# Local attention with two query tiles in two column halves of the array, and sums of squares taken from the loaded rows

## The chip, the cores and the metric

The kernel runs on one core of a Trainium2 chip. The metric is the device time of one execution in microseconds. The kernel before takes 3316.08 us (median of 3 runs, 3313.69 to 3317.71).

## The reference

Two layers of a trunk over 1024 latent tokens with a prefix of 256 context tokens, width 1024, all in float32. Each layer: a modulated RMS norm; one input projection; three mixers side by side (latent attention with 6 heads, a bidirectional state space model, and local attention); an output projection with a gated residual; a second modulated norm and a gated feed-forward part with a convolution. The modulation is silu(c) times the large matrix w_mod.

Two pieces matter here.

The norm: `x * rsqrt(mean(x*x) + eps) * (1 + sc) + sh`, where the mean runs over the 1024 columns of a token.

The local attention: 6 query heads share 2 key-value heads (3 each), head size 64. A query tile of 128 tokens sees its own key tile, the tile before and the one behind (with a mask by distance), the 256 context keys, and a sink: one more logit in the denominator. Context queries see the context alone, in layer 0 only. So `out = sum(p * v) / (sum(p) + exp(sink))` over 5 key tiles (4 at the two ends; 2 for context queries).

## The kernel before, in words

The kernel is one function, `trunk`, written for a scheduler that puts the instructions of each engine in an order by priority and by its own model of time, allocates the tiles, and sets all waits. Tokens are in three chunks: 512, 512, and the 256 context tokens (`CHUNKS`). A helper `mm` issues each matmul, so every product stands at L86; every operation of VectorE and ScalarE stands at L55; transposes at L96. A float32 product is two records of TensorE in the profile (two passes); products of the rounded type fp32r are one.

**Pacing.** Side work runs as generators (`Side`), each advanced by a share of its steps per step of the main work: preparation of the next group, the state space model, the modulation vectors, loads of weights. So side work is tied to the count of attention steps and not to time.

**Local attention** (`swa_steps`). Per chunk and key-value head there is one group: 4 query tiles of 128 tokens, 3 heads side by side as 384 columns. The groups are the context chunk with both heads (layer 0 alone), then (0,0), (0,1), (1,0), (1,1) as (chunk, head). For each query tile and each key tile, a step: two or three products give the scores with keys on the partitions and 384 query columns (`ka`/`qa` and `kb`/`qb` hold rounded parts, so that together they are exact enough; the third adds the mask), ScalarE takes the exponential into `p` (`sp` in the profile), and a function `av`, run two steps later, multiplies with the values: `v1` is 128 keys by 65 columns, of which the last is all ones. Row 65 of the result is the sum of the probabilities. PSUM has 3 banks for scores (`s`), 3 for side work (`b`), 2 for `av`. Behind the last key tile ScalarE copies the 64 rows to `num` and the 65th to `den`, and after the head's last tile `swa_norm` sends the sums through DRAM, adds the sink, inverts, and multiplies.

While a group runs, the next one is prepared (`swa_prep`: transposes, and a maximum of scores per query by VectorE, `smx`); layer 0 also computes a modulation vector (`mod_gen`, `macc`) on VectorE; from step 16 on the mixer's outputs and the output weights are loaded and split into rounded halves (`load_split`). The last group of a layer has no preparation beside it. The output projection (`o`) follows.

**The beginning.** `prep_x(ci)` transposes a chunk of the loaded rows (`xin`) into `xs` (features on partitions). Beside it `norm_stats` squares the transposed tiles on ScalarE, adds them on VectorE (`nb`) and sums over partitions by products with ones (`f<-ones,nb`); GpSimd takes the power -1/2. `use_wm(k)` multiplies the k-th block of w_mod, on TensorE (`pr`) and on VectorE (`x<-wm`, accumulated); `load_wm` loads blocks two ahead, through SP's queue, into 6 buffers. Behind the eighth block `s1_weights(0)` issues three loads of w_in and splits each on ScalarE and VectorE (`wh`, `wl`); there are two buffers for the raw loads. Then the shift `h1` and the scale `A1` are finished, applied, and the first input projections (`tk`) run.

Of the kernel before, what the change touches and what calls it, by code (L numbers as in the profile page):

```python
# [19 lines left out]
D = 1024  # L20
# [12 lines left out]
def trunk(ctx, tc, x, c, ctxt, c_ctx, w_mod, b_mod, norm1, w_in, q_lora_g, w_uq, kv_lora_g, w_ukv,  # L33
# [84 lines left out]

    def stt(out, a, s, b, op0=ALU.mult, op1=ALU.add):
        V.scalar_tensor_tensor(out, a, s, b, op0=op0, op1=op1)  # L120
# [5 lines left out]
    def load_split(hi, lo, raw, srcs, scale=None):  # L126
# [3 lines left out]
        if scale is None:  # L130
            act(hi, raw)
            sub(lo, raw, f32(hi))
        else:
            act(hi, raw, AF.Copy, scale=scale)
            stt(lo, raw, scale, f32(hi), ALU.mult, ALU.subtract)
# [290 lines left out]
    big = [pp.tile([128, 1024], F32, name=f"nb{i}") for i in range(2)]  # L426
    pr = prp.tile([2, 1536], F32, name="pr")
    acc = [[xs[2 * z + q][:, 512:1024] for q in range(2)] for z in range(2)]

    def prep_x(ci):  # L430
        t0, n = CHUNKS[ci]
        st = norm_stats(big, pp, fps, xs, ci, rn[:, ci])
        for k in range(8):
            ps = fps()
            for i in range(n // 128):
# [5 lines left out]
            next(st)  # L441
            yield
        for _ in st:
            yield
# [57 lines left out]
    wS1 = s1_weights(0)  # L502
# [206 lines left out]
    for l in range(2):  # L709
# [969 lines left out]
        def swa_steps(ci, kv):  # L1679
# [9 lines left out]
            for i in range(nt):  # L1689
                t = tt0 + i  # L1690
                kts = [(8, None), (9, None)]
                if ci < 2:
                    kts = [(kt, None if kt == t else (0 if kt < t else 1))
                           for kt in range(max(t - 1, 0), min(t + 2, NL))] + kts
                cs = slice(off + i * 384, off + (i + 1) * 384)
                box = {}
                for e, (kt, mk) in enumerate(kts):
                    ps = cps.tile([128, 512], F32, tag="s", name="s", bufs=3)[:, 0:384]
                    ks = slice(kt * 128, (kt + 1) * 128)
                    mm(ps, ka[:, ks], qa[:, cs], True, False)  # L1700
                    mm(ps, kb[:, ks], qb[:, cs], False, mk is None)
                    if mk is not None:
                        mm(ps, swa["ident_r"], swa["mask_r"][:, mk:mk + 1, :].to_broadcast([128, 3, 128]), False, True)
                    p = swp.tile([128, 384], F32, tag="p", name="sp", bufs=4)
                    act(p, ps, AF.Exp, scale=0.125)

                    def av(e=e, kt=kt, p=p, i=i, box=box, last=e == len(kts) - 1):
# [471 lines left out]
```

## Time and profile before

| | |
|---|---|
| median of the runs | 3316.08 us |
| the profiled execution | 3317.35 us |
| its span | 3315.5 us |
| TensorE, busy | 3216.9 us (97%) |
| VectorE, busy | 2259.5 us (68%) |
| ScalarE, busy | 1160.0 us (35%) |
| GpSimd, busy | 108.1 us (3%) |
| mean granted TensorE clock | 0.985 |

Engines in the rows: PE is TensorE's matmuls, PEld its weight loads, DVE VectorE, ACT ScalarE, POOL GpSimd, SP the queue that issues transfers. A matmul's duration includes its latency, so back-to-back matmuls overlap in the records; their rate is read from the distance of their starts. `x8` in a row of the timeline is 8 instructions in a row, with the time from the first start to the last end.

### The profile page before, as it was taken

To read this page: it belongs to the slowest core of one execution; us is meant where nothing else is said; L and a number is where in the kernel's file an instruction comes from. 1 tells how busy PE (TensorE), PEld (TensorE's weight loads), DVE (VectorE), ACT (ScalarE), POOL (GpSimd) and SP (SyncE) were. 2 spreads that over 40 slices of the span, in tenths; PEclk is the share of its full clock that TensorE was granted. 3 is DMA by queue.
4 is the path that set the end of the run, shared out by engine and by line. 5 is a ranking of instruction groups with operands and counts; after the bars stand their busy time and mean duration, and the time that the engine had idled before them with its cause. 6 is when DMAs were issued, how large, how long until landed. Compare 5 with 4: busy or idle time off the path is not lost.

```text
span 3315.5 us, 41986 instructions
## 1 busy us (share of the span) xinstructions
PE 3216.9 (97%) x15950; PEld 2582.9 (78%) x15950; DVE 2259.5 (68%) x4076; ACT 1160.0 (35%) x2078; POOL 108.1 (3%) x99
## 2 busy tenths in 40 slices
PE   8999699999999999999999999999999999999999
PEld 5897466677878888888888888556668788888888
DVE  7656898885687776666666945887644755565565
ACT  4542344555242222222222553445562322222221
POOL 0220000000000000000000122000000000000000
PEclk9999799999999999999999999999999999999999
DMA  8434221434312222222211445111323112111111
GB/s 268 124 94 109 68 77 49 115 100 147 105 53 76 61 80 65 63 73 65 74 61 36 126 119 141 33 43 40 88 76 113 39 48 61 45 39 58 51 38 58
DMA packets 401892, 263.16 MB, mean 79 GB/s; under 512 B 173711, under 2 KB 370457, under 8 KB 401689
## 3 DMA queue, kind: packets, MB, share of 16 engines
q1 hardware_dynamic: 401042, 260.20, 27.1%
q8 instruction: 126, 2.06, 0.2%
q14 instruction: 77, 0.63, 0.1%
q10 hardware_dynamic: 647, 0.26, 0.0%
HBM read 207.41 MB, written 50.66 MB: 78 GB/s over the span
## 4 chain that ended last, share of the span: by engine, by line
PE 81%; DVE 12%; DMA 3%; ACT 2%; issue 1%; POOL 1%; SPq 1%; DVEq 0%; ACTq 0%; POOLq 0%
PE u L86 32%; PE d L86 11%; PE av L86 6%; PE dx L86 5%; PE o L86 5%; PE f L86 5%; PE tk L86 5%; PE s L86 5%; PE b L86 4%; PE b L96 2%; DVE mx L55 1%; DVE macc L55 1%; DVE cm L55 1%; DMA mw<-in_w_mod_dram 1%; DVE al L55 1%
## 5 line engine op out<-in xcount | busy, mean ns | idle before, releaser
L86 PE MATMUL u<-ah,wh 128*128 128x512 f32 (+1 forms) x1760 | 651.0, 370 | 4.0 <-ACT ah L55 2.2
L86 PE MATMUL u<-al,wh 128*128 128x512 f32 (+1 forms) x1760 | 649.6, 369 | 1.4 <-DVE al L55 1.4
L86 PE MATMUL u<-ah,wl 128*128 128x512 f32 (+1 forms) x1760 | 649.1, 369 | 0.0
L55 ACT ACTIVATE wh<-raw 128x1024 fp32r<-128x1024 f32 (+3 forms) x184 | 189.3, 1036 | 720.4 <-PE d L86 292.2
L55 DVE SCALAR_TENSOR_TENSOR cv<-u,par,cv 128x511 f32<-128x511 f32 (+2 forms) x616 | 326.0, 555 | 135.6 <-ACT cv L55 130.4
L86 PEld LDWEIGHTS u<-ah,wh 128*128 128x128 f32 x1760 | 332.5, 189 | 60.6 <-ACT ah L55 3.1
L86 PEld LDWEIGHTS u<-al,wh 128*128 128x128 f32 x1760 | 332.8, 189 | 57.7 <-DVE al L55 2.0
L86 PEld LDWEIGHTS u<-ah,wl 128*128 128x128 f32 x1760 | 332.6, 189 | 55.5
L55 DVE TENSOR_TENSOR wl<-raw,wh 128x1024 fp32r<-128x1024 f32 (+3 forms) x184 | 218.4, 1191 | 173.0 <-ACT wh L55 171.9
L55 DVE SCALAR_TENSOR_TENSOR x<-d,g,x 128x512 f32<-128x512 f32 (+2 forms) x307 | 209.4, 685 | 109.1 <-PE d L86 108.8
L55 ACT ACTIVATE cv<-u,par,par 128x512 f32<-128x512 f32 (+1 forms) x220 | 159.7, 728 | 323.2 <-PE u L86 320.8
L86 PE MATMUL av<-p,v 128*65 128x512 f32 (+1 forms) x504 | 255.6, 590 | 1.2 <-ACT den L55 0.8
L55 DVE SCALAR_TENSOR_TENSOR macc<-mw,srow,macc 128x256 f32<-128x256 f32 (+1 forms) x364 | 187.2, 539 | 65.4 <-DMA mw<-in_w_mod_dram 64.2
L86 PE MATMUL d<-ah,wh 128*128 128x512 f32 (+2 forms) x614 | 224.5, 366 | 1.3 <-DVE x L55 1.2
L86 PE MATMUL d<-al,wh 128*128 128x512 f32 (+2 forms) x614 | 223.5, 364 | 0.0
L86 PE MATMUL d<-ah,wl 128*128 128x512 f32 (+2 forms) x614 | 223.4, 364 | 0.0
L55 ACT ACTIVATE p<-s 128x512 f32<-128x512 f32 (+1 forms) x252 | 147.4, 586 | 196.5 <-PE s L86 191.8
L55 DVE TENSOR_REDUCE mx<-b 128x1 f32<-128x512 f32 (+1 forms) x300 | 164.1, 586 | 35.6 <-PE b L86 34.2
L86 PE MATMUL s<-qh,kh 97*128 97x512 f32 (+1 forms) x252 | 157.4, 625 | 0.0
L86 PE MATMUL av<-sp,sv 128*65 128x384 f32 x320 | 127.3, 486 | 6.0 <-ACT sden L55 3.3
L55 DVE SCALAR_TENSOR_TENSOR x<-dx,g,x 128x512 f32<-128x512 f32 (+2 forms) x141 | 97.3, 690 | 51.4 <-PE dx L86 51.4
L86 PEld LDWEIGHTS d<-ah,wh 128*128 128x128 f32 x614 | 115.8, 189 | 20.7 <-DVE x L55 2.9
(346 smaller groups left out, 6157.7 us busy)
## 6 DMA issues: line engine op xcount, KB each, us to landing
raw<-in_w_up_dram SPq DMA_DIRECT2D x88, 512.0 KB
mw<-in_w_mod_dram SPq DMA_DIRECT2D x224, 128.0 KB
raw<-in_w_down_dram SPq DMA_DIRECT2D x44, 512.0 KB
mw<-in_w_mod_dram SPq DMA_DIRECT2D x48, 256.0 KB
wm<-in_w_mod_dram SPq DMA_DIRECT2D x16, 512.0 KB
xd<-x SPq DMA_DIRECT2D x32, 256.0 KB
raw<-in_w_in_dram SPq DMA_DIRECT2D x14, 512.0 KB
sqd<-sqb SPq DMA_DIRECT2D x36, 192.0 KB
```

Of the source, the lines that this page charges most:

```text
L55: return fn(out, *args, **kw)
L86: PE.matmul(out, lhsT, rhs, start=start, stop=stop)
L96: PE.transpose(out, in_, ident[0:p, 0:p])
```

## The change

Three edits.

1. `swa_steps` takes the query tiles of a group in pairs. For each place e in the two lists of key tiles it computes the scores of both tiles; the product with the values of the first tile goes to rows 0 to 63 of one PSUM bank, that of the second to rows 64 to 127 (64 columns of values each, without the ones). The sums of probabilities are made apart: `tot` is added up per query tile, the first tile's on VectorE, the second's on GpSimd, and behind the last key tile two products with ones give both denominators in another `av` bank. Where one list is longer, its last place goes alone. The buffers of `p` go from 4 to 5.
2. `prep_x` no longer uses `norm_stats`. ScalarE squares the loaded rows with a running sum along the row (`accum_out`), at k = 0 and k = 4; behind k = 4 two small operations and the power give the norm.
3. The loads of `s1_weights(0)` are issued behind block 3 of w_mod instead of behind the last; their splits are kept in a list and issued behind block 6.

```diff
@@ -116,6 +116,8 @@
         else:
             (eng or V).tensor_scalar(out, a, s1, s2, op0=op0, op1=op1)
 
+    later_splits = None
+
     def stt(out, a, s, b, op0=ALU.mult, op1=ALU.add):
         V.scalar_tensor_tensor(out, a, s, b, op0=op0, op1=op1)
 
@@ -127,9 +129,10 @@
 
         for dst, src in srcs:
             nc.sync.dma_start(out=dst, in_=src)
-        if scale is None:
-            act(hi, raw)
-            sub(lo, raw, f32(hi))
+        if later_splits is not None:
+            later_splits.append(lambda: split(hi, lo, raw))
+        elif scale is None:
+            split(hi, lo, raw)
         else:
             act(hi, raw, AF.Copy, scale=scale)
             stt(lo, raw, scale, f32(hi), ALU.mult, ALU.subtract)
@@ -424,23 +427,32 @@
     stt(th, th, 1.0, cv, ALU.add, ALU.mult)
     ts(srow.rearrange("p k j -> p j k"), th, 0.5)
     big = [pp.tile([128, 1024], F32, name=f"nb{i}") for i in range(2)]
+    xss = pp.tile([128, 2, NT], F32, name="xss")
     pr = prp.tile([2, 1536], F32, name="pr")
     acc = [[xs[2 * z + q][:, 512:1024] for q in range(2)] for z in range(2)]
 
     def prep_x(ci):
+
         t0, n = CHUNKS[ci]
-        st = norm_stats(big, pp, fps, xs, ci, rn[:, ci])
+        nt = n // 128
         for k in range(8):
+            if k % 4 == 0:
+                for i in range(nt):
+                    act(big[1][:, (i % 2) * 512:(i % 2) * 512 + 512], xin[t0 // 128 + i, k // 4], AF.Square,
+                        accum_out=xss[:, k // 4, t0 // 128 + i:t0 // 128 + i + 1])
             ps = fps()
-            for i in range(n // 128):
+            for i in range(nt):
                 tr(ps[:, i * 128:(i + 1) * 128], xin[t0 // 128 + i, k // 4][:, k % 4 * 128:k % 4 * 128 + 128])
             if k % 2:
                 V.tensor_copy(xs[k][:, t0:t0 + n], ps[:, :n])
             else:
                 act(xs[k][:, t0:t0 + n], ps[:, :n])
-            next(st)
-            yield
-        for _ in st:
+            if k == 4:
+                v = pp.tile([128, 4], F32, tag="nv", name="nv", bufs=2)
+                sl = slice(t0 // 128, t0 // 128 + nt)
+                add(v[:, :nt], xss[:, 0, sl], xss[:, 1, sl])
+                ts(v[:, :nt], v[:, :nt], 1.0 / D, EPS)
+                rsqrt_pool(rn[:, ci, 0:nt], v[:, :nt], nt)
             yield
 
     def use_wm(k):
@@ -499,7 +511,13 @@
         use_wm(k)
         if k + 2 < 8:
             load_wm(k + 2)
-    wS1 = s1_weights(0)
+        if k == 3:
+            later_splits = []
+            wS1 = s1_weights(0)
+            first_splits, later_splits = later_splits, None
+        if k == 6:
+            for fn in first_splits:
+                fn()
     load_x(1)
     load_x(2)
     rb0 = pp.tile([128, 256], F32, name="rb0")
@@ -1686,34 +1704,64 @@
             num, den = pair["snum"], pair["sden"]
             o = kv * 64
             tt0, nt = CHUNKS[ci][0] // 128, CHUNKS[ci][1] // 128
-            for i in range(nt):
-                t = tt0 + i
-                kts = [(8, None), (9, None)]
-                if ci < 2:
-                    kts = [(kt, None if kt == t else (0 if kt < t else 1))
-                           for kt in range(max(t - 1, 0), min(t + 2, NL))] + kts
-                cs = slice(off + i * 384, off + (i + 1) * 384)
+
+            def scores(i, kt, mk):
+                ps = cps.tile([128, 512], F32, tag="s", name="s", bufs=3)[:, 0:384]
+                ks, cs = slice(kt * 128, (kt + 1) * 128), slice(off + i * 384, off + (i + 1) * 384)
+                mm(ps, ka[:, ks], qa[:, cs], True, False)
+                mm(ps, kb[:, ks], qb[:, cs], False, mk is None)
+                if mk is not None:
+                    mm(ps, swa["ident_r"], swa["mask_r"][:, mk:mk + 1, :].to_broadcast([128, 3, 128]), False, True)
+                p = swp.tile([128, 384], F32, tag="p", name="sp", bufs=5)
+                act(p, ps, AF.Exp, scale=0.125)
+                return p
+
+            for i0 in range(0, nt, 2):
+
+                kts = []
+                for t in (tt0 + i0, tt0 + i0 + 1):
+                    r = [(8, None), (9, None)]
+                    if ci < 2:
+                        r = [(kt, None if kt == t else (0 if kt < t else 1))
+                             for kt in range(max(t - 1, 0), min(t + 2, NL))] + r
+                    kts.append(r)
+                ne = max(len(r) for r in kts)
+                tot = [None, None]
                 box = {}
-                for e, (kt, mk) in enumerate(kts):
-                    ps = cps.tile([128, 512], F32, tag="s", name="s", bufs=3)[:, 0:384]
-                    ks = slice(kt * 128, (kt + 1) * 128)
-                    mm(ps, ka[:, ks], qa[:, cs], True, False)
-                    mm(ps, kb[:, ks], qb[:, cs], False, mk is None)
-                    if mk is not None:
-                        mm(ps, swa["ident_r"], swa["mask_r"][:, mk:mk + 1, :].to_broadcast([128, 3, 128]), False, True)
-                    p = swp.tile([128, 384], F32, tag="p", name="sp", bufs=4)
-                    act(p, ps, AF.Exp, scale=0.125)
-
-                    def av(e=e, kt=kt, p=p, i=i, box=box, last=e == len(kts) - 1):
-                        if "av" not in box:
+                for e in range(ne):
+                    ps_ = []
+                    for z in range(2):
+                        if e >= len(kts[z]):
+                            continue
+                        kt, mk = kts[z][e]
+                        p = scores(i0 + z, kt, mk)
+                        ps_.append((z, kt, p, e == len(kts[z]) - 1))
+                        eng = G if z else V
+                        if e == 0:
+                            tot[z] = p
+                        else:
+                            q = tot[z]
+                            if e == 1:
+                                tot[z] = swp.tile([128, 384], F32, tag=f"tot{z}", name="stot")
+                            add(tot[z], q, p, eng)
+                        if z == 0 and len(kts[1]) > e:
+                            yield lambda: None
+
+                    def av(e=e, ps_=ps_, box=box, tot=tot, i0=i0, ne=ne):
+                        if e == 0:
                             box["av"] = cps.tile([128, 512], F32, tag="av", name="av", bufs=2)[:, 0:384]
                         av = box["av"]
-                        mm(av[0:65], v1[:, kt, :], p, e == 0, last)
-                        if last:
-                            sl = slice(i * 128, (i + 1) * 128)
-                            act(num[o:o + 64, :, sl], av[0:64, :].rearrange("p (h q) -> p h q", h=3))
-                            act(den[o:o + 1, :, sl], av[64:65, :].rearrange("p (h q) -> p h q", h=3))
-                            if kv == 1 and i == nt - 1:
+                        for z, kt, p, last in ps_:
+                            mm(av[64 * z:64 * z + 64], v1[:, kt, 0:64], p, e == 0, last)
+                        if e == ne - 1:
+                            dn = cps.tile([128, 512], F32, tag="av", name="sdn", bufs=2)[:, 0:384]
+                            for z in range(2):
+                                mm(dn[64 * z:64 * z + 64], ones[:, 0:64], tot[z])
+                            for z in range(2):
+                                sl = slice((i0 + z) * 128, (i0 + z + 1) * 128)
+                                act(num[o:o + 64, :, sl], av[64 * z:64 * z + 64, :].rearrange("p (h q) -> p h q", h=3))
+                                act(den[o:o + 1, :, sl], dn[64 * z:64 * z + 1, :].rearrange("p (h q) -> p h q", h=3))
+                            if kv == 1 and i0 == nt - 2:
                                 swa_norm(ci, num, den)
                     yield av
 
```

## Rows read from the trace of the kernel before

**Rows 1.** The page: busy time of the engines, and the chain that ended last.
```profile
PE 3216.9 (97%) x15950; PEld 2582.9 (78%) x15950; DVE 2259.5 (68%) x4076; ACT 1160.0 (35%) x2078; POOL 108.1 (3%) x99
...
PE 81%; DVE 12%; DMA 3%; ACT 2%; issue 1%; POOL 1%; SPq 1%; DVEq 0%; ACTq 0%; POOLq 0%
```
**Rows 2.** Busy by stretch: length, PE, PEld, DVE, ACT, POOL; clock, DMA, GB/s.
```profile
690.00:772.00 82.00, 78.70 (x397) 59.34 (x396) 70.70 (x168) 50.76 (x110) 0.00 (x0) 1.00 0.40 120
772.00:799.40 27.40, 26.87 (x111) 16.82 (x110) 8.73 (x19) 18.32 (x39) 0.00 (x0) 1.00 0.22 64
2377.00:2457.00 80.00, 79.63 (x389) 59.65 (x388) 51.71 (x108) 50.89 (x105) 0.00 (x0) 1.00 0.25 74
2457.00:2483.40 26.40, 24.23 (x100) 15.21 (x98) 4.90 (x5) 18.01 (x37) 0.00 (x0) 1.00 0.33 95
...
50.00:100.00 50.00, 45.78 (x301) 42.56 (x300) 43.89 (x106) 29.55 (x85) 4.93 (x5) 0.91 0.66 208
```
**Rows 3.** TensorE's timeline, layer 0, last group: start us, length, instruction.
```profile
742.49 0.33 PE L86 MATMUL s<-qb,kb 128*128 128x384 f32 x1
742.66 0.27 PE L96 MATMUL b<-ident,snm 128*12 128x128 f32 x1
742.77 0.81 PE L86 MATMUL av<-sp,sv 128*65 128x384 f32 x2
...
743.59 0.34 PE L86 MATMUL s<-qb,kb 128*128 128x384 f32 x1
743.76 0.34 PE L86 MATMUL s<-mask_r,ident_r 128*128 128x384 f32 x1
743.94 0.81 PE L86 MATMUL av<-sp,sv 128*65 128x384 f32 x2
```
**Rows 4.** The tile sp: durations in ns (min/median/max), first and last start.
```profile
L86 PE MATMUL av<-sp,sv x320: 483/485/537, 683.6 to 2483.4; 128*65 128x384 f32 x160
L55 ACT ACTIVATE sp<-s x160: 465/491/502, 682.1 to 2482.0; 128x384 f32<-128x384 f32 x160
```
**Rows 5.** TensorE's timeline: products with 64 rows; transposes with all rows.
```profile
367.83 0.60 PE L86 MATMUL b<-cv,bb 64*16 64x128 f32 x8
...
368.37 0.64 PE L96 MATMUL b<-ident,qn 128*96 128x128 f32 x4
...
689.68 1.03 PE L96 MATMUL b<-ident,q 128*128 128x128 f32 x8
```
**Rows 6.** VectorE: groups in 690 to 772 (busy, mean ns | idle); a stretch.
```profile
L55 DVE TENSOR_TENSOR snum<-snum,sden 128x512 f32<-128x512 f32 x3 | 1.9, 685 | 0.0
L55 DVE TENSOR_TENSOR snum<-snum,sden 128x256 f32<-128x256 f32 x3 | 1.2, 418 | 0.0
...
660.00:683.00 23.00, 23.00 (x113) 16.11 (x113) 21.83 (x55) 8.99 (x19) 0.00 (x0) 1.00 0.26 77
```
**Rows 7.** GpSimd: groups over the whole span.
```profile
L102 POOL TENSOR_TENSOR rinv<-ssq,mhalf 128x12 f32<-128x12 f32 x28 | 71.7, 2561 | 167.3 <-DVE ssq L55 167.3
L1257 POOL MEMSET Sg<- 64x4 f32 x16 | 1.6, 100 | 0.6
```
**Rows 8.** The beginning: two stretches, chain, groups of 0 to 100, timeline.
```profile
20.00:25.00 5.00, 4.01 (x22) 2.02 (x20) 3.82 (x7) 1.23 (x2) 0.00 (x0) 1.00 0.97 388
25.00:30.00 5.00, 5.00 (x19) 1.60 (x19) 4.58 (x12) 0.00 (x0) 1.18 (x1) 1.00 0.55 155
...
33.53 6.59 DMA wm<-in_w_mod_dram
...
L55 DVE TENSOR_TENSOR nb<-nb,nb 128x512 f32<-128x512 f32 x12 | 7.9, 685 | 2.1 <-ACT nb L55 2.0
...
L86 PE MATMUL f<-ones,nb 128*128 128x2 f32 x40 | 5.0, 243 | 1.0 <-DVE nb L55 1.0
...
L55 ACT ACTIVATE nb<-x x24: 402/624/633, 9.2 to 88.5; 128x512 f32<-128x512 f32 x16, 128x256 f32<-128x256 f32 x8
...
42.94 1.05 DVE L55 TENSOR_TENSOR wl<-raw,wh 128x864 fp32r<-128x864 f32 x1
```

## The prediction

> **What bounds the kernel now.** Begin with the page: TensorE is busy 97% of the span and holds 81% of the chain that ended last [rows 1]. So a change pays where it shortens TensorE's stream, as long as no other engine is full there. The parts touched are the local attention (682 to 799.4 us in layer 0, 2377 to 2483.4 us in layer 1) and the first 100 us. Next the table of stretches [rows 2]: read for each which engine comes second. TensorE is nearly full in all four attention stretches, but VectorE has 70.7 of 82 us in layer 0 at 690 to 772 and 51.7 of 80 us in layer 1 at 2377 to 2457; the last quarter of each stage has little VectorE and much ScalarE (18.3 of 27.4, 18.0 of 26.4 us). Last the order of TensorE's work [rows 3]: one step (one key tile of one query tile) with a mask takes 743.94 - 742.77 = 1.17 us; its three one-pass streams start 0.17 to 0.18 us apart, so the product with the values keeps 1.17 - 3 x 0.175 = 0.645 us. It is the dear half of the step: two records of 0.485 us latency each [rows 4], 320 records for 160 products, 103.2 us in all.
>
> **Products and sums, TensorE.** A latent group (one key-value head, four query tiles) has 5+5+5+4 = 19 products, 19 x 0.645 = 12.3 us. After the change the tiles go in pairs with lists of 4 and 5, or 5 and 5: 10 slots of up to two half-array products. Each pair adds one slot for its denominators (ones times the summed probabilities): 12 slots. Is a slot 0.645 us or twice that? No row has column halves, but one has row halves: products with 64 rows, alternating between the two halves, go 8 in 0.60 us; a record of 128 columns lasts 0.27 us [rows 3], so they start (0.60 - 0.27)/7 = 0.05 us apart, against (1.03 - 0.27)/7 = 0.11 us for full-array float32 passes of the same 128 columns [rows 5]. So two float32 products, both passes of each, ran side by side on different parts. I take a column slot at 0.645 us, the same as one product now; the bounds are 0.645 and 1.29. Then a group saves 12.3 - 12 x 0.645 = 4.5 us, eight groups 36, the two context groups (4 products to 3 slots each) 1.3: 37 us of TensorE's stream.
>
> Changing the shape of the array twice per slot: around the 12-column transpose the starts are 0.17 and 0.11 us apart, just its neighbour's and its own stream, so no gap [rows 3]; I take 0, and as the upper end 0.09 us, from the 64-row products: the last of the eight starts at 367.83 + 0.60 - 0.27 = 368.16 and the next full-array pass at 368.37, 0.21 where 0.11 is the stream [rows 5]. The Trainium skill (TensorEngine Tiling (Array Packing), Key Properties) says that changing the mode drains TensorE; the 64-row rows agree, the 12-column rows do not. By the page some 84 visits to the halves would cost 2 x 0.09 us each, 15 us of TensorE, and the sum below would lose about 8 of them, where TensorE sets the pace.
>
> **What the sums cost elsewhere.** Probabilities are now added per query tile: even tile on VectorE, odd tile on GpSimd, one add fewer than key tiles. VectorE's two-input operations in this stage take 0.685 us for 512 columns and 0.418 for 256 [rows 6]; 384 lie half way, 0.55 us. A latent group has 3+4 or 4+4 on VectorE, so three groups 22 x 0.55 = 12.1 us. For GpSimd there is no such row: its two-input operations (powers) are 2.56 us for 12 columns, memsets 0.10 us [rows 7]; these are the bounds, and I take about 1 us, between them, because a plain add is nearer the memset than the power. ScalarE has the same exponentials (0.491 us [rows 4]) and as many evacuations; only now four of these come in a row at a pair's end. Nothing else moves: the count of steps that paces loads, modulation and the next group's preparation is again 19 per group.
>
> **The stretches, one by one** [rows 2]. Layer 0, 690 to 772 (three groups beside preparation and modulation): TensorE 78.7 - 13.5 = 65.2, but VectorE 70.7 + 12.1 = 82.8 us. It would be full; the fullest stretch before it has 21.8 of 23 us, 95% [rows 6], so 82.8 to 87; I take 85, 3 us longer than now. Layer 0, 772 to 799.4 (one group, little beside it): TensorE 26.9 - 4.5 = 22.4, ScalarE 18.3: about 23.4, 4 less. Layer 1, 2377 to 2457 (no modulation): TensorE 79.6 - 13.5 = 66.1, VectorE 51.7 + 12.1 = 63.8; two engines nearly even do not pack perfectly, I take 70, 10 less. Layer 1's last group: TensorE 24.2 - 4.5 = 19.7, ScalarE 18.0: 21.4, 5 less. Together -16 us, though TensorE loses 37: VectorE eats the rest in layer 0. The output projection that follows is on TensorE alone and simply starts earlier.
>
> **The beginning.** The sums of squares leave VectorE (12 adds of 512 columns, 7.9 us, and 6 of 256) and TensorE (40 products with ones, 5.0 us of busy time); the eight squares of a chunk stay on ScalarE, now read from the loaded rows with a running sum, at about the 0.62 us that 512 columns cost now [rows 8]. ScalarE has 29.6 of 50 us at 50 to 100 [rows 2], so these hide; if the running sum costs 0.2 us more each, 20 of them are 4 us there, still hidden. Early on VectorE frees w_mod's buffers: transfers fall from 388 GB/s at 20 to 25 us to 155 at 25 to 30, because no buffer is free while VectorE adds squares. With these adds gone, up to 5 x (0.388 - 0.155) = 1.2 MB move earlier, some 3 us. Against it, two of the three w_in loads (128 x 864 float32, 0.44 MB, each) pass in SP's queue ahead of the last w_mod loads, whose landing ends the 6.59 us wait at 33.53 [rows 8]: 0.9 MB, 2.3 us at 0.388 MB/us. These two about cancel; bounds -3 and +3. The third w_in load still needs a buffer that the first split frees, now at step 6 and not after step 7. What is left is the two splits of 1.05 us that stand on VectorE between the reductions at 42 to 46 us, ahead of A1: 2.1 us sooner, in the wait for w_mod, where VectorE is idle. I take -3 us. At 50 to 100 us TensorE has 45.8 of 50 us [rows 2]: 24 of the 40 products with ones, 3 us, go. Beginning: -6 us, between +2 and -9.
>
> **Sum.** The profiled execution took 3317.35 us (span 3315.5), 1.3 us above the median of the runs, 3316.08. 3317.35 - 16 - 6 = 3295 us. Own range 3287 to 3304.
>
> **Rivals.**
> 1. The column halves run one after the other (the slower side). Then a group has 19 + 4 = 23 products of 0.645, 2.6 us more; eight groups 21, context 2.6, less 6 at the beginning: about 3335. It decides from a slot price of (103.2 + 6)/102 = 1.07 us on. For: no row shows column halves. Against: the row halves overlap fully [rows 5].
> 2. The overlap is half: of first and second passes only one pair meets, 0.96 us a slot, and back-to-back slots somewhat less. TensorE saves about 13 us, the stretches 4 plus 6: 3307.
> 3. TensorE waits at each pair's end for the odd tile's last add. Behind the last score come two products and two scores, 2 x 0.645 + 0.7 = 2.0 us; the exponential takes 0.5, so a GpSimd add up to 1.4 us is covered; at 2.5 us, its upper bound, 18 pair ends wait 1.1 us each: 20 us, so 3315. Behind the waiting product on TensorE stand all next scores, and for them wait the exponentials.
> 4. VectorE is held while GpSimd adds. In the full stretch of layer 0 each 0.1 us held per add is 24 x 0.1 = 2.4 us on the end; at 0.4 us it is 10: 3305. No row has the two side by side. The Trainium skill (GPSIMD Engine Reference, 1. Specifications) says that the two share SBUF interfaces and contend when VectorE reads two inputs, which would speak against this change; no row of the kernel before shows it. The same page (3.1 Elementwise) has 4497 ns for an add of 2048 columns, an estimate of 0.84 us for 384, by which rival 3 would not wait at all.
> 5. It goes better: layer 0's VectorE work, paced by steps, slides into the slack of the last group, and the beginning reaches its bound. Layer 0 then gains 5 more and the rest 8: 3282.
>
> **How the numbers follow.** Forecast 0.48, rivals in order 0.12, 0.06, 0.16, 0.08, 0.10. Differences under 0.2% (6.6 us) can't be told from none, so faster means below 3309.4 and slower above 3322.7. Faster: the forecast, 5, nearly all of 2 and 4, and a little of 3: 0.68. Slower: rival 1 and the tail of 3: 0.16. Same: 0.16. The range for 8 in 10 leaves out rival 1 and the far tail below: 3280 to 3318.
>
> **What would show it.** Two halves' products with starts a few ns apart and a pair every 0.32 us show the overlap; starts 0.32 us apart, one by one, show rival 1. Stretches of layer 0 no shorter, with VectorE above 95%, and of layer 1 shorter by 10 and 5 us show the limit. Waits of TensorE on GpSimd show rival 3; VectorE's operations longer than 0.55 and 0.685 us show rival 4. In the beginning VectorE's A1 should come near 43 us and the w_mod loads have no gap at 25 us. The forecast is wrong if a slot costs over 1 us, or if layer 0 loses more than layer 1 gains.

## The result, and the profile after

The changed kernel takes 3343.18 us (median of 4 runs, 3339.83 to 3350.09), the kernel before in the same session 3316.89 us (4 runs). The ratio is 1.0086, 95% interval [1.0072, 1.0101]: slower by 0.86%, where 0.6% faster was forecast. The profiled execution of the changed kernel is the slowest of its four, 3350.09 us; the single times below are from it, the changes in per cent from all runs.

The page of the changed kernel answers to the first of [rows 1], the busy time of the engines.

```profile
PE 3240.3 (97%) x15982; PEld 2555.6 (76%) x15982; DVE 2298.5 (69%) x4123; ACT 1159.3 (35%) x2094; POOL 176.6 (5%) x161
```

TensorE was to lose 37 us of its stream and is busy 23.4 us longer than in [rows 1]. The stretches of the local attention, in the columns of [rows 2] (length, TensorE, weight loads, VectorE, ScalarE, GpSimd, granted clock, DMA), layer 0 first:

```profile
690.00:797.00 107.00, 98.64 (x425) 55.02 (x421) 86.40 (x188) 52.95 (x113) 24.04 (x23) 0.96 0.30 89
797.00:824.00 27.00, 22.84 (x98) 11.18 (x99) 16.12 (x28) 14.01 (x30) 7.77 (x7) 0.82 0.22 65
2390.00:2488.00 98.00, 97.80 (x447) 57.72 (x445) 65.65 (x131) 49.97 (x107) 23.98 (x22) 1.00 0.20 60
2488.00:2516.50 28.50, 25.60 (x109) 12.31 (x107) 16.47 (x23) 19.96 (x41) 10.24 (x8) 0.94 0.24 70
```

The reader is to see two different things. In layer 1 TensorE is full, and it simply takes longer. In layer 0 it is busy for only 98.6 of 107 us, then 22.8 of 27 at a clock of 0.82: there it also waits. Measured from the first product with the values to the first product of the output projection, layer 0 takes 142.9 us (115.3 before) and layer 1 110.8 (101.0 before): +27.6 and +9.8. At the beginning the first `tk` product starts at 56.6 us instead of 49.5, but the first score product at 300.3 instead of 302.9. These three make 34.8 us, the span grew by 32.8.

**A visit to the halves.** TensorE's timeline (start us, length, instruction), the stretch that answers to [rows 3]:

```profile
741.53 0.33 PE L86 MATMUL b<-bandm,ident_r 128*128 128x384 f32 x1
741.70 0.34 PE L86 MATMUL s<-mask_r,ident_r 128*128 128x384 f32 x1
741.88 0.28 PE L86 MATMUL b<-ka,qa 128*128 128x256 f32 x1
742.08 0.54 PE L86 MATMUL av<-sp,sv 128*64 128x384 f32 x1
742.09 0.54 PE L86 MATMUL sdn<-stot,ones 128*64 128x384 f32 x1
742.45 0.49 PE L86 MATMUL av<-sp,sv 128*64 128x384 f32 x1
742.46 0.49 PE L86 MATMUL sdn<-stot,ones 128*64 128x384 f32 x1
742.88 0.44 PE L86 MATMUL b<-ka,qa 128*128 128x384 f32 x1
743.16 0.34 PE L86 MATMUL b<-bandm,ident_r 128*128 128x384 f32 x1
743.42 0.86 PE L86 MATMUL sdn<-stot,ones 128*64 128x384 f32 x2
744.21 0.45 PE L86 MATMUL s<-qa,ka 128*128 128x384 f32 x1
```

The overlap is there: two products on different halves start 0.01 us apart (742.08 and 742.09, second passes at 742.45 and 742.46). But the visit to the halves has a price at both ends. Going in, the record of 384 columns at 743.16 is followed after 0.26 us, where such a record streams in 0.175 (741.53 to 741.88 are two): 0.085. The first pass takes 0.37 us instead of the 0.32 of a pass before (half of 0.645): 0.05. Going out, 742.46 to 742.88 is 0.42 instead of 0.32: 0.10. The first full-array record takes 0.28 (742.88 to 743.16) instead of 0.175: 0.105. Together 0.34 us a visit, that is, for each run of half products between two full-array records. What goes with it, the weight loads of the same stretch show (PEld: the loads of TensorE's weights):

```profile
741.70 0.19 PEld L86 LDWEIGHTS b<-ka,qa 128*128 128x128 f32 x1
742.08 0.13 PEld L86 LDWEIGHTS av<-sp,sv 128*64 128x64 f32 x1 [0.19 <-issue]
742.09 0.13 PEld L86 LDWEIGHTS sdn<-stot,ones 128*64 128x64 f32 x1
742.13 0.14 PEld L86 LDWEIGHTS av<-sp,sv 128*64 128x64 f32 x1
742.14 0.14 PEld L86 LDWEIGHTS sdn<-stot,ones 128*64 128x64 f32 x1
742.88 0.19 PEld L86 LDWEIGHTS b<-ka,qa 128*128 128x128 f32 x1 [0.60 <-DVE smx L55]
```

The load for the record of 741.88 starts at 741.70, beside the record before it. The loads for the first halves, and for the first full record behind them, start only with their own record: across the change of the array's shape, weights are not loaded ahead. It is so throughout: at all 65 ways in and 65 ways out of layer 0 the load starts within 0.005 us of its record, and elsewhere 0.17 us ahead at the median. In the kernel before, at [rows 3], the loads for the transpose with 12 columns (its record starts at 742.66) and for the product with 65 (742.77) start ahead, beside the record before:

```profile
742.49 0.09 PEld L96 LDWEIGHTS b<-ident,snm 128*12 128x12 f32 x1
742.66 0.24 PEld L86 LDWEIGHTS av<-sp,sv 128*65 128x65 f32 x2
```

No run changes the loads alone, so that the late load is the cause is read from these rows and not shown apart; that the visit has its price is shown by e4 below.

The second loss is in the same timeline: at 743.42 a half product goes alone (two passes, x2). Of the 118 visits that the trace shows (65 in layer 0, 53 in layer 1), 58 hold one product, 51 hold two and 9 hold more. The two halves of a place, written one behind the other, stand apart in TensorE's order, with scores between them. So the visits fill 129 slots where the forecast had 102.

The sum by these counts: 118 x 0.34 = 40 us for the visits, (129 - 160) x 0.645 = -20 us for the slots, so +20 us of TensorE. By layer, against 84 and 76 products before: layer 0 has 65 visits and 70 slots, +22.1 - 9.0 = +13.1; layer 1 has 53 and 59, +18.0 - 11.0 = +7.0. That is most of layer 1's +9.8; the granted clock there (0.94 over the last 28.5 us, 1.00 in [rows 2]) takes up to 1.7 us more. Layer 0 has 14.5 us more, and the table of TensorE's waits for 680 to 824 us has most of it (us in total, times, longest):

```profile
PE b L96 <- DVE snm L55: 8.8, 3, 4.8
PE sdn L86 <- DVE stot L55: 3.5, 2, 3.4
```

TensorE waits for VectorE: three times for the next group's maxima, which come late because the adds stand among them, and twice for a sum. The granted clock (0.96, then 0.82, where [rows 2] have 1.00 throughout) takes up to 107 x 0.04 + 27 x 0.18 = 9 us more.

The adds themselves are as forecast in the median, but not at the long end (ns, min/median/max, layer 0; the first row VectorE, the second GpSimd):

```profile
L55 DVE TENSOR_TENSOR stot<-stot,sp x22: 532/552/1366, 696.5 to 822.4; 128x384 f32<-128x384 f32 x22
L102 POOL TENSOR_TENSOR stot<-stot,sp x22: 996/1008/1299, 697.4 to 821.2; 128x384 f32<-128x384 f32 x22
```

Where VectorE's long operations stand, GpSimd adds. VectorE's timeline at one of them, and GpSimd's:

```profile
788.39 1.68 DVE L55 SCALAR_TENSOR_TENSOR macc<-mw,srow,macc 128x256 f32<-128x256 f32 x2
```

```profile
788.79 1.00 POOL L102 TENSOR_TENSOR stot<-stot,sp 128x384 f32<-128x384 f32 x1 [2.43 <-ACT sp L55]
```

Two `macc` operations, 0.475 us each elsewhere, take 1.68: the second lasts 1.28, past the end of GpSimd's add. In layer 0 (680 to 830 us) 69 of VectorE's 223 operations overlap an add on GpSimd; against the median of the same operation in the kernel before and in e8 below, neither of which has these adds, they are 9.4 us longer in all, 13 of them by over 0.25 us (12 of these read two tiles). The other 154 are not longer. So VectorE carries 32 adds of 0.552 us, 18 us, and 9 us of being held.

### The profile page after: what moved, and what is told of

Its sections match the earlier page's. It is cut to its first block, busy times and chain, and to the rows that moved or that the text cites. A ratio compares the mean times of both kernels' runs of the same rounds, so it can differ in the third digit from the quotient of the medians.

```text
span 3348.3 us, 42287 instructions
## 1 busy us (share of the span) xinstructions
PE 3240.3 (97%) x15982; PEld 2555.6 (76%) x15982; DVE 2298.5 (69%) x4123; ACT 1159.3 (35%) x2094; POOL 176.6 (5%) x161
## 4 chain that ended last, share of the span: by engine, by line
PE 83%; DVE 10%; DMA 3%; ACT 2%; issue 1%; POOL 0%; SPq 0%; DVEq 0%; ACTq 0%; POOLq 0%
PE u L86 32%; PE d L86 11%; PE av L86 6%; PE s L86 5%; PE dx L86 5%; PE o L86 5%; PE f L86 5%; PE b L86 5%; PE tk L86 5%; PE b L96 2%; DVE mx L55 1%; DVE macc L55 1%; DVE cm L55 1%; DMA mw<-in_w_mod_dram 1%; DVE sv L55 1%
## 5 line engine op out<-in xcount | busy, mean ns | idle before, releaser
L86 PE MATMUL b<-kh,qh 96*128 96x512 f32 (+1 forms) x300 | 116.1, 440 | 14.4 <-DVE ql L55 6.7
```

Of the source, the lines that this page charges most:

```text
L86: PE.matmul(out, lhsT, rhs, start=start, stop=stop)
```

## The experiments

Ratios are to the kernel before, run on the same chip in the same session, with 95% intervals. "Layer 0" and "layer 1" are the times from the first product with the values to the output projection in one profiled execution.

| kernel | ratio | layer 0, us | layer 1, us |
|---|---|---|---|
| before | 1 | 115.3 | 101.0 |
| changed | 1.0086 [1.0072, 1.0101] | 142.9 | 110.8 |
| e1, early edits alone | 0.9986 [0.9978, 0.9995] | 117.1 | 101.8 |
| e2, attention alone | 1.0111 [1.0097, 1.0124] | 143.2 | 110.3 |
| e4, 64 columns, no pairs | 1.0133 [1.0118, 1.0149] | 138.4 | 121.8 |
| e5, pairs tied | 1.0061 [1.0049, 1.0073] | 132.5 | 107.9 |
| e8, attention without adds | 1.0080 [1.0068, 1.0092] | 135.1 | 105.4 |
| e9, tied, without adds | 1.0030 [1.0019, 1.0042] | 124.4 | 101.1 |
| e10, tied, adds on GpSimd | 1.0093 [1.0078, 1.0109] | 138.9 | 109.4 |
| e14, tied, VectorE lighter | 1.0050 [1.0037, 1.0064] | 126.3 | 107.5 |
| e15, e9 with VectorE lighter | 0.9998 [0.9989, 1.0006] | 116.3 | 101.0 |

**e1 and e2: each part alone.** No new code: the hunks of the diff, split.

> Only the early edits (squares from the loaded rows with a running sum, the three w_in loads issued behind block 3, their splits behind block 6); the attention is that of the kernel before. Theory (a queue): the third w_in load stands in SP's queue ahead of the last two w_mod loads and waits there for the first split; in the changed kernel it went out at 39.7 us and the last w_mod loads at 41.2 and 41.7 us, where before they went out at 33.5. I expect the last w_mod load to leave near 41 us, the first tk product near 56 us where it was 49.5, and a time 4 to 8 us above the kernel before: 3321 to 3325. Rival (my forecast): 6 us less than before, 3311, and all of the loss is the attention's.

Measured 0.9986, 4.6 us less. The delay is real (the first `tk` product at 54.0 us), but the inference from it was wrong: it is more than won back by 100 us (the 200th `tk` product starts at 93.2 us, 98.9 before), and my forecast for this part, -6, was about right.

> Only the attention's edit; the beginning is that of the kernel before. Theory (the visit's price): each visit of TensorE to the column halves costs 0.34 us beside its products (0.085 until the first half's weights start to load, 0.05 for that load, 0.10 before the next full array's weights start, 0.107 for that load), and the order has 118 visits: 40 us, against 33 products fewer in line (160 to 127 places), 21 us. So +19 us of TensorE, some 12 of them in layer 0 and 8 in layer 1, and 3335 to 3340 in all. Rival (VectorE and the sums): layer 0 loses up to 12 us because VectorE is full there, layer 1 gains 10 as forecast, and the time is that of the kernel before, 3317.

Measured 1.0111, some 37 us more, so all of the loss is here. Layer 1, +9.3 against the 8 expected, is in the main the visits; layer 0, +27.9, is over twice the 12 expected, since its waits for VectorE (8.8 and 4.6 us in its table) were left out. The rival, a gain in layer 1, is out.

**e4: the price of a visit by itself.**

```diff
-                        mm(av[0:65], v1[:, kt, :], p, e == 0, last)
+                        mm(av[0:64], v1[:, kt, 0:64], p, e == 0, last)
-                            act(den[o:o + 1, :, sl], av[64:65, :]...)
+                            act(den[o:o + 1, :, sl], av[0:1, :]...)
```

> The kernel before with one change: the product with the values takes 64 columns of values instead of 65, so that it runs on a half of the array; the denominators are left out (a row of the numerators stands in for them). Nothing is paired and nothing is added on VectorE or GpSimd; 160 products in 147 visits. Theory (visit's price): 147 x 0.342 = 50 us more of TensorE, 3355 to 3367 in all. Rival (the loss comes from the pairs, from their sums, or only from the second half's columns): no change, 3317.

Measured 1.0133, 44 us more, for one column less. The timeline has the same two ends as the changed kernel:

```profile
735.55 0.28 PE L86 MATMUL b<-ka,qa 128*128 128x256 f32 x1
735.76 0.86 PE L86 MATMUL av<-sp,sv 128*64 128x384 f32 x2
736.55 0.44 PE L86 MATMUL s<-qa,ka 128*128 128x384 f32 x1
736.83 0.33 PE L86 MATMUL s<-qb,kb 128*128 128x384 f32 x1
```

From the half's start to the next full record 0.79 us instead of 0.645, then 0.28 for a record of 0.175. 44 us over 147 visits is 0.30 us each (0.27 to 0.34 by the interval), near the 0.34 of the timeline. The price needs neither pairs nor sums nor the second half.

**e3 and e5: the halves kept together.** First with an atomic section around the products of a place; then with dependences and priority:

```diff
                         for z, kt, p, last, _ in ps_:
+                            with tc.high_priority():
                                 m = mm(av[64 * z:64 * z + 64], v1[:, kt, 0:64], p, e == 0, last)
+                            behind(m, ps_[-1][4])
```

Here `behind` makes a product wait for the given instruction as well, the last exponential of the place; the denominators' products wait likewise for both last adds.

> As the attention alone, but the two half products of a place, and the two of the denominators, are kept next to each other on TensorE (an atomic section): 102 visits instead of 118, and of 58 visits with one lone product only the 8 with an odd key tile are left. Theory (visit's price): TensorE spends 102 x (0.645 + 0.342) = 101 us on them, 2.5 less than the 103.2 of the kernel before and 21 less than the attention alone; where VectorE does not hold it back, 3315 to 3322. Rival (VectorE and the sums set the time): the adds are the same, so the time is that of the attention alone, about 3337.

Measured 1.0559 [1.0542, 1.0576], 185 us more, and it tells nothing of the pairs: with the section the weight loads stand, and TensorE's products of the attention wait for work that they do not need, the load of the output weights and the modulation vector. From its table of waits (690 to 900 us):

```profile
PEld av L86 <- issue: 44.7, 41, 2.8
...
PE sdn L86 <- DMA raw<-in_w_out_dram: 5.3, 1, 5.3
PE av L86 <- DVE macc L55: 4.9, 4, 1.9
```

> The attention's edit alone, with the two half products of a place tied together: the first one is made to wait for the second one's exponential too, and both stand ahead of other ready work in TensorE's order (no barrier, unlike the atomic section). The order now has 75 visits for the same 196 half products, one of them lone, in 102 places. Theory (visit's price): 102 x 0.645 + 75 x 0.342 = 91 us of TensorE, where the attention alone has 127 x 0.645 + 118 x 0.342 = 122: 31 less, so 3322 to 3330, the upper end if VectorE's waits in layer 0 stay. Rival (the sums on VectorE and GpSimd set the time): the adds are the same, only layer 1 can gain, about 3341.

Measured 1.0061: 15 to 17 us less than the loose pairs, where 31 were expected. The trace has 75 visits and 102 slots, as expected. That lone halves cost is shown. The time is nearer the rival's 3341 than the theory's range, but the rival's reason is out, since layer 0 gained most (10.7 us, layer 1 2.4). The rest went into waits, in layer 0 (680 to 815 us, first two rows) as without the tie, and in layer 1 for GpSimd's sums (2380 to 2510 us, last):

```profile
PE b L96 <- DVE snm L55: 10.1, 3, 5.0
PE sdn L86 <- DVE stot L55: 3.4, 1, 3.4
```

```profile
PE sdn L86 <- POOL stot L102: 2.8, 6, 0.8
```

**e6: fewer visits.** `av` runs for two places at once, `sp` has 9 buffers, and the tag `n2` has 1 buffer instead of 2.

> As the tied pairs, but two places go in one visit (probabilities in 9 buffers instead of 5; the loaded keys and queries have one buffer instead of two to make room): 40 visits for the same 196 half products, again 102 places' worth. Theory (visit's price): 102 x 0.645 + 40 x 0.342 = 79.5 us of TensorE, 12 less than the tied pairs and 43 less than the attention alone: 3310 to 3320, the upper end where VectorE holds layer 0. Rival (the sums set the time): no gain over the tied pairs.

Measured 1.0121 [1.0106, 1.0135], 20 us more than the tied pairs: both theories missed. The visits fell to about half, 40, but only some 10 of the lost 24 us between the two profiled executions lie from a layer's first local score to its output projection (2 in layer 0, 8 in layer 1). There TensorE now waits for four exponentials where it waited for two (second row, 2390 to 2526 us), and in layer 0 still for the maxima (first row, 680 to 825 us):

```profile
PE b L96 <- DVE snm L55: 10.8, 3, 5.5
```

```profile
PE s L86 <- ACT sp L55: 3.9, 2, 2.8
```

Another 12 us lie ahead of the local attention of the two layers, where there are no pairs. The single `n2` buffer was changed with it and not tried alone, so what these are due to is not settled.

**e7: column quarters.** As e5, with two products of 32 columns for each of 64.

> As the tied pairs, but each half product is cut into two of 32 columns of values, so that a place is four products in four column quarters; the denominators take 32 columns each. 78 visits. In the kernel before the 12-column transposes (a 32-column part of the array) start without any gap; so theory A (only 64-column parts cost a visit): no price, 102 x 0.645 = 66 us of TensorE, 3300 to 3312. Theory B (every change of the parts costs 0.34 us, quarters run side by side as halves do): like the tied pairs, 3322 to 3332. Theory C (quarters do not all run side by side): up to 80 x 0.645 = 52 us more, 3375.

Measured 1.0083 [1.0070, 1.0096]; theory B, though above its range; the 7 us over e5 are not explained. Its timeline:

```profile
734.81 0.33 PE L86 MATMUL s<-qa,ka 128*128 128x384 f32 x1
735.08 0.85 PE L86 MATMUL av<-sp,sv 128*32 128x384 f32 x8
735.86 0.44 PE L86 MATMUL s<-qb,kb 128*128 128x384 f32 x1
736.14 0.34 PE L86 MATMUL b<-ka,qa 128*128 128x384 f32 x1
```

Eight records (four products of two passes) take 0.78 us, as two do in e4: the quarters run side by side, and the ends cost the same (0.27 in, 0.28 behind).

**e8 and e9: the adds left out**, with loose and with tied pairs.

```diff
-                        eng = G if z else V
...
-                            add(tot[z], q, p, eng)
+                        tot[z] = p
```

> The attention's edit alone with the adds left out: the denominators' products take the last probabilities of each query tile instead of their sum (and ScalarE an exponential instead of a copy of them, of the same size, so that they stay finite). VectorE and GpSimd have none of the adds. 110 visits in 125 places. Theory (visit's price sets most of it): TensorE 4 us less than with the adds, its waits for VectorE in layer 0 (14.7 us, and some 5 us of low clock behind them) go: 3328 to 3336, so still 10 to 18 over the kernel before, all of it the visits. Rival (the sums are all of the loss): 3318.

> The tied pairs with the adds left out, as in the attention without adds (the denominators' products take the last probabilities, ScalarE an exponential of them). 75 visits, 102 places, nothing added on VectorE and GpSimd. Theory (visits, lone halves and sums are the whole of the loss, and the sums cost most once TensorE has got shorter): TensorE 102 x 0.645 + 75 x 0.342 = 91.4 us against 103.2 before, no waits for sums: 3306 to 3318. Rival (parts simply add, and a part of the loss is not named): tied pairs less the 10 us that the adds cost beside the loose pairs, 3328. If above 3330, the tie itself makes waits.

e8 measured 1.0080: the adds cost some 10 us of the 37, not the 17 to 25 expected and far from the rival's 35; layer 0 is 8.1 us shorter than in e2, layer 1 4.9. e9 measured 1.0030, 10 us over the kernel before: the theory's range (to 3318, ratio about 1.000) missed, its rival hit. The four kernels e2, e8, e5 and e9 add up: the tie is worth 17 us either way (1.0111 to 1.0061 and 1.0080 to 1.0030), the adds 10. In e9 layer 1 is even with the kernel before and layer 0 still 9.1 us longer, though TensorE has less to do.

**e10: all adds on GpSimd** (`eng = G`).

> The tied pairs with all adds on GpSimd (124 instead of 62), none on VectorE. If VectorE's 62 adds make TensorE wait for the next group's maxima in layer 0 (10 us, and 5 to 7 us of low clock behind), these go; against it the last adds of a pair's two tiles now follow each other on GpSimd, 2 x 1.01 us, so that at 18 pair ends TensorE waits up to 1 us longer: 3330 to 3342, with the wait for maxima under 3 us in the table of waits and that for GpSimd's sums over 10. Rival (VectorE is late for another reason than its adds): the wait for maxima stays at 10 us, and 3345 to 3355.

Measured 1.0093, 11 us more than with both engines and just above the range. The waits for `snm` are gone from layer 0, so VectorE's adds did make them and the rival is out; the sums took their place, with 5.6 us instead of over 10 (680 to 820 us):

```profile
PE sdn L86 <- POOL stot L102: 5.6, 6, 2.5
PE av L86 <- ACT sp L55: 3.6, 2, 3.0
```

With twice the adds on GpSimd, 29 of VectorE's operations in layer 0 are held by over 0.25 us, 19 us in all (13 and 9.4 in the changed kernel).

**e13 to e15: VectorE lighter in layer 0**, by work that has nothing to do with the attention:

```diff
-                    else:
+                    elif (nm, l) != ("A2", 0):
                         stt(acc[z], wt, srow[:, k, z:z + 1], acc[z])
```

> The kernel before with VectorE made lighter in layer 0's local attention alone: the accumulation of layer 0's A2 vector (44 operations of 0.475 us, 21 us) is left out but for its first term, its loads stay. A control: TensorE sets the pace of the kernel before, so 3312 to 3317, a gain of at most 4 us. If VectorE were holding the kernel before too: 10 us or more less.

> The tied pairs with the same 21 us of VectorE left out. If VectorE is what holds layer 0 once the adds have joined its work there (waits for maxima 10 us, for sums 3.4 us, low clock behind them some 5): 12 to 16 us less than the tied pairs, layer 0 from 510 to 497 us from its first score to its output projection, 3322 to 3326 (ratio 1.002). Rival (it is the chain of the next group's preparation, step by step, however light VectorE is): 3 us at most, 3335 (1.005).

> The tied pairs without adds (ratio 1.0030) with the same 21 us of VectorE left out. If VectorE holds layer 0 there too: layer 0 from 504 to 490 us and a time below the kernel before, 3306 to 3312 (ratio 0.998). Rival (the chain of preparation and the steps' own waits): 3320 or more.

e13 measured 0.9994 [0.9985, 1.0003]: the kernel before is not held by VectorE there. e14 measured 1.0050, 4 us less than e5: the wait for maxima falls from 10.1 to 2.1 us, but TensorE then waits 5.1 us for exponentials; the rival's number, by another wait than the rival named. e15 measured 0.9998, 10 us less than e9, and layer 0 8.1 us shorter, between the two numbers: VectorE did hold it there, less than expected. Even so the halves gain nothing: no adds, pairs tied, VectorE light, and the time is that of the kernel before.

**e11 and e12: the beginning taken apart.** e11 has the squares alone; e12 all early edits, with the third w_in load behind the last w_mod loads:

```diff
-            wS1 = s1_weights(0)
+            wS1 = load_movs(S1_COLS, w_in[0], 6, 3)
+        if k == 5:
+            wS1 += load_mov(S1_COLS, w_in[0], 6, 2)
             first_splits, later_splits = later_splits, None
```

> Only the squares from the loaded rows with a running sum; w_in loads and splits as in the kernel before, attention as before. If the squares are all of the beginning's gain: 3311 to 3314, the first tk product at or before 49.5 us. If the early w_in loads and splits give it: 3317.

> The early edits, with the third w_in load issued behind the last w_mod loads, so that these do not stand behind it in SP's queue. If the delay of the first tk product (54.0 us with the early edits, 49.5 before) is lost time: the last w_mod loads leave near 36 us, the first tk product comes near 50, and 3307 to 3309. If what is late there is won back by TensorE's clock and a fuller stream at 50 to 100 us: 3312, as with the early edits.

Both measured 0.9979 [0.9970, 0.9987], 3307.99 and 3306.58 us, the two fastest kernels of the study. SP's queue in the changed kernel (first three rows) and in e12 (start us, length, transfer):

```profile
35.85 0.91 SPq L416 DMA_DIRECT2D wm<-in_w_mod_dram  x2
39.71 1.40 SPq L131 DMA_DIRECT2D raw<-in_w_in_dram  x3
41.21 1.73 SPq L416 DMA_DIRECT2D wm<-in_w_mod_dram  x2
```

```profile
32.41 1.85 SPq L418 DMA_DIRECT2D wm<-in_w_mod_dram  x4
36.26 1.87 SPq L131 DMA_DIRECT2D raw<-in_w_in_dram  x3
```

In the changed kernel the third w_in load stands ahead of the last two w_mod loads until the first split has freed its buffer, and these go out at 41 us; in e12 they go out from 32.4. e12's first `tk` product starts at 50.5 us, 3.5 ahead of e1's. The times differ by 0.07%, inside the intervals: that the late loads cost anything is not shown. What the squares give is, by a place that the forecast did not name. The stretch 80 to 100 us in the kernel before, in e11 and in the changed kernel (in e1 and e12 TensorE is busy 20.0 and 19.7 us of it):

```profile
80.00:100.00 20.00, 16.52 (x111) 15.67 (x110) 18.28 (x54) 11.01 (x37) 2.86 (x3) 0.87 0.41 113
```

```profile
80.00:100.00 20.00, 19.00 (x136) 18.17 (x135) 19.79 (x68) 12.44 (x43) 4.53 (x4) 1.00 0.45 119
```

```profile
80.00:100.00 20.00, 20.00 (x151) 19.22 (x150) 19.30 (x57) 11.42 (x37) 3.89 (x3) 1.00 0.51 142
```

TensorE loses 3.5 of 20 us in the kernel before, at a clock of 0.87, because the sums of squares (VectorE's adds to 89 us, the products with ones at 90.6) make the context chunk's norm late; with the squares from the loaded rows it loses 1.0 us or less, at 1.00.

## Why the prediction was wrong, point by point

- **What bounds the kernel**: right. TensorE sets the pace; e13 confirms that VectorE does not in layer 0's local attention.
- **A slot of two halves at 0.645 us**: half right. The two products of a visit overlap fully, 0.01 us apart, so rival 1 came nearest to the time (3335, measured 3343) for a wrong reason: that is luck.
- **The step that failed: "Changing the shape of the array twice per slot ... I take 0, and as the upper end 0.09 us".** It is 0.34 us per visit, and e4 shows it alone (44 us for 147 visits). The 118 visits cost 40 us where the sum had nothing. The 12-column transposes without a gap were the wrong neighbour, and the 64-row rows showed one end of the price only; I had measured the distance of starts and not looked at when the weights were loaded. What the Trainium skill says (TensorEngine Tiling (Array Packing), Key Properties), that changing the mode drains TensorE, agrees with the trace (0.10 us on the way out before the full array's load starts); I weighed it with the 0.09 of the row; at 0.34 its 84 visits would have taken 29 of the 37 us. The 12-column transposes pay nothing where their weights are loaded ahead (742.49 for 742.66); why they are and those of the halves are not is open.
- **"12 slots" per group, 102 in all**: wrong by the order. The forecast took the halves of a place to stay together; 58 of 118 visits held a lone product. The 27 slots too many are 17 us. The tie (e5), which takes these and 43 visits away, brings 15 to 17 us where the counts give 31.
- **The adds**: VectorE's 0.55 us (0.552 measured) and GpSimd's 1 us (1.008) were right. What they cost was named (VectorE full in layer 0), and e8 and e5 with e9 put it at 10 us. It shows as waits for the next group's maxima, not as a full engine: VectorE is busy 86.4 of 107 us.
- **The stretches**: layer 0 -1 forecast, +27.6 measured; layer 1 -15 forecast, +9.8 measured. The visits and the lone halves are 20 us of this by the counts; the waits for VectorE 12, the low clock up to 11. The prediction's own sign of being wrong, layer 0 losing more than layer 1 gains, came in a stronger form: both lose.
- **Rival 3** (TensorE waits for GpSimd's last add): not in the changed kernel's table for layer 0, but in e10's, 5.6 us.
- **Rival 4** (VectorE held while GpSimd adds): it happens, at 9.4 / 32 = 0.29 us per GpSimd add in layer 0, under the 0.4 of that rival; beside the visits it is a small part. What the Trainium skill says (GPSIMD Engine Reference, 1. Specifications), that the two contend when VectorE reads two inputs, agrees with the held operation shown and with 12 of the 13.
- **The beginning**: -6 forecast, -4.6 measured for e1 [-7.3, -1.7], and for partly other reasons, so the near number is in part luck. The late w_mod loads were missed: I saw that the third w_in load needs a freed buffer, but not that the last two w_mod loads queue behind it.
- **What is left**: e15 has some 12 us less of counted TensorE work than the kernel before and the same time in both layers. Its trace has some 10 of them. TensorE's waits in the two layers are 9.8 us, 3.5 more than before, the longest of them ahead of the last group of layer 1, for the transfer that brings that group's maxima into `qb` (first row, 2375 to 2493 us). And the granted clock is at the lower of its two levels (1.2 instead of 2.4 GHz) for some 7 us from 776.7 us and again from 2459.4 us, where TensorE is busy 17.6 of 20 us (760 to 780) and 17.4 of 20 us (2440 to 2460): 0.91 to 0.92 over 760 to 800 us, 0.86 over 2460 to 2482 (second row), where the kernel before has 1.00; that takes up to 6.5 us. No run took these two away.

```profile
PE s L86 <- DMA qb<-snr: 2.4, 1, 2.4
```

```profile
2460.00:2482.00 22.00, 21.39 (x89) 11.38 (x90) 4.46 (x5) 13.28 (x27) 0.00 (x0) 0.86 0.31 91
```

## What to carry to other kernels

Price a part-array product with both of its ends, and count visits and not products: a visit's 0.34 us takes half of the 0.645 that a paired place saves here, and a half product that goes alone only pays. What two instructions gain by standing together must be enforced in the order, and paid for in waits. When a new sum is put beside existing work, look for who waits for that work next, not only at the engine's mean share.

## What the runs showed of the hardware that was not expected

- Weights are not loaded ahead across a change between full-array and part-array products: in the changed kernel the first half's load starts 0.26 us after the start of a 384-column record, not beside it, and the full array's load 0.42 us after the last half's start, at all 130 changes in layer 0 within 0.005 us of the record that needs it. e4 and e7 have the same distances of starts, with one product of 64 columns or four of 32.
- Four products in column quarters, two passes each, take 0.78 us, one product in a half 0.79, each up to the start of the next full-array record.
- An add of 384 float32 columns takes 1.008 us on GpSimd and 0.552 on VectorE, and a VectorE operation of 0.475 us lasted 1.28 beside one.
- In all thirteen profiles with the old sums of squares TensorE is busy 16.4 to 16.5 of the 20 us from 80 to 100; in the four without, 19.0 to 20.0.
